# A two-layer encoder trunk on one core: attention issued two sub-steps at a time, with one run of dense products between clusters, and five smaller moves around it

## The chip, the cores and the metric

The kernel runs on one core of a Trainium2 chip. The time is device microseconds (us) of one execution; the median of several executions is what counts. Before the change three timed executions took 2770.01, 2779.59 and 2778.19 us, a median of 2778.19 us.

The engines are TensorE (PE in the profile, its weight loads PEld), VectorE (DVE), ScalarE (ACT), GpSimd (POOL) and the queue of DMA issues (SP).

## The reference, cut to what matters

There are 2048 tokens, 1024 channels, 16 heads of 64. Layer A is a gated pooling mixer, layer B a strictly causal stick-breaking attention; each is followed by an output projection and a gated embedding add.

```python
# layer A
h = rms_norm(x, a_norm);  u, z = split(h @ a_w_in)
x = x + ((group_map(trailing_mean(u) - u) * scale) * silu(z)) @ a_w_out
x = x + (p[0] @ ple_w[0]) * sigmoid(x @ ple_gate_w[0])
# keys and values, once; then layer B
k, v = split(rms_norm(x, kv_norm) @ w_kv);  k = rms_norm_per_head(k)
q, z = split(rms_norm(x, b_norm) @ b_w_in); q = rms_norm_per_head(q)
keep[t, s] = 1 - sigmoid(q_t . k_s / 8)           # s < t
a[t, s]    = sigmoid(q_t . k_s / 8) * prod(keep[t, j] for s < j < t)
o = a @ v
x = x + (o * silu(z)) @ b_w_out
out = x + (p[1] @ ple_w[1]) * sigmoid(x @ ple_gate_w[1])
```

## The kernel before, in words

**Dense products.** Every float32 operand is held as a high and a low part, and each product is three matmuls per 128-row block of the contraction (high by high, high by low, low by high; `product`, line 267, `kvq`, line 632). One product of 128 output rows by 512 tokens is 24 matmuls of 128x512, and it gathers in one of two banks (tile `psd`). Weights come in units of 512 KB (tile `wpair`), nine buffers in a ring. A unit is asked for when the unit nine places ahead of it in `plan` is given back (`give_back`, line 214). On its first use a weight is read raw (`wraw`) and split by ACT (line 176) and DVE (line 177); `keep` stores the split pair in DRAM (`once`), and later uses read the pair. In a chunk, `plan_kvq(s, b)` (line 228) plans half b of the query, key and value weights, eight units of 512 output columns each; the pair is kept if s >= b, so half 0 is raw in chunk 0, and half 1 is raw in chunks 0 and 1.

**Stages.** The tokens go in four chunks of 512. For each chunk the dense stream (`stream`, line 826) runs the mixer, its output projection, the gate, then z of layer B (`gate_z`) and two halves of q, k and v (`kvq`). After the fourth chunk come the output projections and gates of layer B (`post`) for three chunks; that of the last chunk runs alone at the end.

**Attention.** It is laid out in 160 slots (chunk of queries, head, chunk of keys), each of four sub-steps. A sub-step has a front, a turn and a gather. `front` (line 880) makes 128x512 logits with two matmuls (`psl`), ACT takes the sigmoid (line 889), DVE scans the running product along the keys (line 893). `turn` (line 900) transposes one 128-key block of four such tiles into a bank `psa` (two banks), ACT copies the high part `at` (line 908), DVE subtracts the low part (line 910). `gather` (line 912) multiplies both parts by the values (`pso`). The turn of a slot comes `LAG_T` sub-steps behind its front, the gather `LAG_G` behind. The transposes of finished query and key rows (`finish`, line 702, tile `pst`) take the same two `psa` banks.

**What sets the order.** From the first mark on, PE's instructions are held in the order of the program. The loop at line 991 emits, per sub-step, a turn and a front, then half of the step's dense matmuls (`fill`), then a gather and the other half. `rate` (line 965) sets the dense matmuls per sub-step by the chunk of queries: 26.8, 12.9, 7.4 and 5.7. Loads and late steps are hung on a clock that counts dense matmuls (`after`). The other engines' order is set by a scheduler with a timeline of its own. All loads and nearly all stores go through SP's queue, in order.

**Start.** Chunk 0's mixer begins before the sums of squares of x are known: `square_first` (line 413) takes a square on ACT and adds it over channels with four one-column matmuls (`pst<-ones,sq`, eight records in the trace); `norm_first` takes the root and spreads it with four transposes.

## Time and profile before

| | before |
|---|---|
| timed executions, us | 2770.01, 2779.59, 2778.19 |
| the profiled execution's own time, us | 2769.64 |
| its span, first to last instruction, us | 2767.9 |
| mean granted TensorE clock | 0.991 |
| PE busy, us (share) | 2719.8 (98%) |
| DVE, ACT, POOL busy | 65%, 44%, 27% |
| moved by DMA | 684.27 MB, mean 247 GB/s |
| matmul records | 13406 |
| attention, first to last sigmoid, us | 393.1 to 2661.1 |

PE's matmuls overlap, and their ends are modelled; the distance from one start to the next is the price of a matmul, and the duration is not. The granted clock of PE stands in the page as a digit per slice and in the table of windows as a share: 1.00 is full speed, and stretches at half speed pull it down. Busy time of PE at half speed counts as busy.

### The profile page before, as it was taken

The page shows a single profiled execution, that of the slowest core. Times are in us where ns is not written, and L with a number is a line of the kernel's source. Part 1 is how long each engine was busy: PE and PEld are TensorE (multiplying, and loading weights), DVE is VectorE, ACT ScalarE, POOL GpSimd, SP SyncE. Part 2 cuts the span into 40 slices and gives each one's busy share as a digit, 9 for nine tenths or more (in the row PEclk, how much of TensorE's full clock was granted, in tenths as well). Part 3 has the DMA queues.
Part 4 walks back from the last instruction along what each step waited for, and adds up shares of the span by engine and source line. Part 5 has one row for each costly group of instructions (what it writes and reads, how often), then busy time and mean ns, then how long its engine had stood idle before and what let it go on. Part 6 is the DMA issues. An engine that isn't in the chain of part 4 may idle for free.

```text
span 2767.9 us, 37889 instructions
## 1 busy us (share of the span) xinstructions
PE 2719.8 (98%) x13406; PEld 2243.3 (81%) x13406; DVE 1811.1 (65%) x2367; ACT 1229.2 (44%) x2412; POOL 759.0 (27%) x617
## 2 busy tenths in 40 slices
PE   9999989999999999999999999999999999999999
PEld 7878868888877888887778888888888888888887
DVE  5636445644445776655558878776787887887842
ACT  4435543233444334454444445554555444445431
POOL 1345432224432332354223212212211201111101
PEclk8999999999999999999999999999999999999999
DMA  6779888687789878877897676778577765766655
GB/s 223 259 279 346 302 245 279 223 270 246 251 289 321 289 256 272 289 263 249 275 304 235 218 228 208 250 219 265 176 244 239 240 205 184 250 209 211 223 170 184
DMA packets 311306, 684.27 MB, mean 247 GB/s; under 512 B 49222, under 2 KB 81990, under 8 KB 311116
## 3 DMA queue, kind: packets, MB, share of 16 engines
q1 hardware_dynamic: 310540, 681.05, 73.9%
q8 instruction: 106, 1.74, 0.3%
q10 hardware_dynamic: 576, 0.79, 0.1%
q14 instruction: 84, 0.69, 0.1%
HBM read 493.45 MB, written 179.90 MB: 243 GB/s over the span
## 4 chain that ended last, share of the span: by engine, by line
PE 86%; DMA 8%; DVE 2%; ACT 1%; POOL 1%; SPq 1%; issue 1%; ACTq 0%; DVEq 0%; POOLq 0%
PE psd L47 59%; PE psl L47 9%; PE pso L47 9%; PE psa L51 8%; DMA wpair<-once 3%; DMA wraw<-in_w_kv_dram 1%; DMA wraw<-in_b_w_q_dram 1%; PE pst L51 1%; DMA vs<-vr 1%; PE pst L47 1%; DMA kd<-hl 0%; DMA wraw<-in_gate_a_dram 0%; ACT wpair L176 0%; DVE wpair L177 0%; DMA xin<-in_x_dram 0%
## 5 line engine op out<-in xcount | busy, mean ns | idle before, releaser
L893 DVE TENSOR_TENSOR_SCAN pp<-pp,floor 128x512 f32<-128x512 f32 (+3 forms) x640 | 772.9, 1208 | 28.9 <-ACT pp L889 26.9
L910 DVE TENSOR_TENSOR at<-psa,at 128x512 fp32r<-128x512 f32 (+3 forms) x640 | 387.6, 606 | 432.6 <-ACT at L908 429.9
L908 ACT CAST at<-psa 128x512 fp32r<-128x512 f32 (+3 forms) x640 | 333.3, 521 | 726.8 <-PE psa L51 706.1
L47 PE MATMUL psd<-wpair,x 128*128 128x512 f32 x2304 | 615.2, 401 | 25.4 <-DMA wpair<-once 12.8
L47 PE MATMUL psd<-x,wpair 128*128 128x512 f32 x2304 | 606.5, 394 | 1.8 <-ACT x L157 1.6
L47 PEld LDWEIGHTS psd<-wpair,x 128*128 128x128 f32 x2304 | 425.2, 190 | 121.3 <-DMA wpair<-once 20.3
L47 PEld LDWEIGHTS psd<-x,wpair 128*128 128x128 f32 x2304 | 427.1, 188 | 90.0 <-ACT x L157 2.0
L47 PE MATMUL psd<-xp,wpair 128*128 128x512 f32 x1536 | 395.5, 398 | 0.4 <-DVE wpair L177 0.2
L47 PE MATMUL pso<-at,vv 128*128 128x512 f32 (+3 forms) x1280 | 360.9, 363 | 0.0
L889 ACT ACTIVATE pp<-psl 128x512 f32<-128x512 f32 (+3 forms) x640 | 344.6, 538 | 8.7 <-PE psl L47 4.4
L51 PE MATMUL psa<-ident,pp 128*128 128x128 f32 x2176 | 343.7, 273 | 3.0 <-DVE at L910 1.5
L51 PEld LDWEIGHTS psa<-ident,pp 128*128 128x128 f32 x2176 | 275.2, 140 | 84.7 <-DVE pp L893 2.3
L47 PEld LDWEIGHTS psd<-xp,wpair 128*128 128x128 f32 x1536 | 286.9, 191 | 59.6 <-DVE wpair L177 1.2
L47 PE MATMUL psl<-kk,qa 128*128 128x512 f32 (+3 forms) x640 | 283.7, 443 | 0.0
L47 PEld LDWEIGHTS pso<-at,vv 128*128 128x128 f32 x1280 | 240.3, 188 | 53.6
L47 PE MATMUL psl<-kk,qb 128*128 128x512 f32 (+3 forms) x640 | 233.8, 365 | 0.0
L47 PE MATMUL psd<-og,wpair 128*128 128x512 f32 x744 | 208.9, 394 | 0.0
L47 PE MATMUL psd<-mp,wpair 128*128 128x512 f32 x768 | 193.0, 392 | 0.0
L47 PEld LDWEIGHTS psd<-mp,wpair 128*128 128x128 f32 x768 | 142.5, 188 | 29.3
L47 PEld LDWEIGHTS psd<-og,wpair 128*128 128x128 f32 x744 | 137.6, 188 | 28.7
L610 POOL TENSOR_TENSOR xj<-x 128x512 f32<-128x512 f32 x64 | 106.2, 1665 | 149.1 <-DVE sg L621 144.8
L158 POOL TENSOR_TENSOR x<-xr,x 128x512 fp32r<-128x512 f32 x32 | 43.1, 1349 | 329.6 <-ACT x L157 297.1
(118 smaller groups left out, 2655.6 us busy)
## 6 DMA issues: line engine op xcount, KB each, us to landing
wpair<-once SPq DMA_DIRECT2D x468, 512.0 KB
once<-wpair SPq DMA_DIRECT2D x116, 512.0 KB
kk<-kd SPq DMA_DIRECT2D x160, 256.0 KB
vv<-vd SPq DMA_DIRECT2D x160, 256.0 KB
wpair<-wf SPq DMA_DIRECT2D x48, 512.0 KB
once<-kp SPq DMA_DIRECT2D x36, 512.0 KB
qd<-hl SPq DMA_DIRECT2D x64, 256.0 KB
qa<-qd SPq DMA_DIRECT2D x64, 256.0 KB
```

The source lines that it names most:

```text
L47: return held_in_order(nc.tensor.matmul(*a, **k))
L51: return held_in_order(nc.tensor.transpose(*a, **k))
L158: lo.tensor_tensor(out=pr[:, 1], in0=src, in1=f(pr[:, 0]), op=ALU.subtract)
L610: G.tensor_tensor(out=xj, in0=f(x1[o][:, 0]), in1=f(x1[o][:, 1]), op=ALU.add)
L889: A.activation(out=pp[:, r0:], in_=ps[:, :w], func=AF.Sigmoid, scale=-1.0)
L893: V.tensor_tensor_scan(out=pp[:, r0:][:, ::-1], data0=pp[:, r0:][:, ::-1], data1=least, initial=1.0 if st["diag"] else st["carry"][j], op0 ...
L908: A.copy(out=at[:, 0, cs], in_=pt[:, cs])
L910: return lambda: V.tensor_tensor(out=at[:, 1, cs], in0=pt[:, cs], in1=f(at[:, 0, cs]), op=ALU.subtract)
```

## The change

1. The attention loop runs in steps of two sub-steps. Each step emits four gather matmuls, eight transposes, four logit matmuls in one cluster, then DVE's two subtractions and two scans, then one run of `2 * rate` dense matmuls. `LAG_T, LAG_G` are 3 and 4 double steps. The gather of a turned block comes one double step behind its turn; values are loaded two double steps ahead of their first gather. 44 dense matmuls instead of 24 go ahead of the first step.
2. In `kvq`, token blocks 0 and 1 share the second half of block 0's and the first half of block 1's matmuls, as blocks 2 and 3 did before.
3. In chunks 1 and 2, z of layer B goes between the two halves of q, k, v (before: ahead of both; chunk 3 had it between already). There the token norm is then made in `kvq`, and the first two banks are copied out until it is known.
4. The transposes of query and key rows get a time: 28 dense matmuls after the last row, at least 9 apart, and in the attention only inside a dense run, from its 7th matmul to its third last.
5. In the mixer of chunk 0 the squares begin at matmul 15 of the second product instead of 0, five of the eight fall into the third product, and the root and its spreading are apart.
6. The query tile with its halves swapped (`qb`) is made by two ACT copies from `qa`, 14 dense matmuls after its load or at the first front; before, two DMAs read it from DRAM.

The number of PE instructions is the same. ACT has 130 more (128 of them the copies to `qb`), SP 128 fewer.

In the last part of the attention (queries of chunk 3), on PE, one sub-step stood so before (`psa` transposes, `psl` logits, `pso` gathers, `psd` dense):

```order
L51 MATMUL psa<-ident,pp 128x128 x4
L47 MATMUL psl<-kk,qa 128x512
L47 MATMUL psl<-kk,qb 128x512
L47 MATMUL psd<-ple,wpair 128x512 x3
L47 MATMUL pso<-at,vv 128x512 x2
L47 MATMUL psd<-x_22654,wpair 128x512 x3
```

and a double step stands so now:

```order
L47 MATMUL pso<-at,vv 128x512 x4
L51 MATMUL psa<-ident,pp 128x128 x8
L47 MATMUL psl<-kk,qa 128x512
L47 MATMUL psl<-kk,qb 128x512
L47 MATMUL psl<-kk,qa 128x512
L47 MATMUL psl<-kk,qb 128x512
L47 MATMUL psd<-x_22925,wpair 128x512 x3
L47 MATMUL psd<-x_23041,wpair 128x512 x3
L47 MATMUL psd<-x_23140,wpair 128x512 x3
L47 MATMUL psd<-x_23256,wpair 128x512 x2
```

Four short dense runs in two sub-steps have become one of eleven or twelve.

In the mixer of chunk 0, on PE, the first one-column matmuls move back by 15 dense matmuls (`uh` and `ul` belong to the folded weights ahead of it):

```order
 L47 MATMUL psd<-wpair,ul 128x256
 L47 MATMUL psd<-wpair,uh 128x256
-L47 MATMUL psd<-xp,wpair 128x512 x25
+L47 MATMUL psd<-xp,wpair 128x512 x40
 L47 MATMUL pst<-ones,sq 128x1 x4
 L47 MATMUL psd<-xp,wpair 128x512 x3
```

The eight rounds of four such matmuls and three dense ones follow as before.

In the first block of q, k, v of chunk 0, on PE, where x_2151, x_2176, x_2224 and x_2303 are the first four contraction blocks of the activations, token block 1 now begins between the last four contraction blocks of token block 0:

```order
 L47 MATMUL psd<-wpair,x_2224 128x512 x3
 L47 MATMUL psd<-wpair,x_2303 128x512 x3
+L47 MATMUL psd<-wpair,x_2151 128x512 x3
 L47 MATMUL psd<-wpair,x_2349 128x512 x3
+L47 MATMUL psd<-wpair,x_2176 128x512 x3
 L47 MATMUL psd<-wpair,x_2435 128x512 x3
+L47 MATMUL psd<-wpair,x_2224 128x512 x3
 L47 MATMUL psd<-wpair,x_2482 128x512 x3
+L47 MATMUL psd<-wpair,x_2303 128x512 x3
 L47 MATMUL psd<-wpair,x_2570 128x512 x3
-L47 MATMUL psd<-wpair,x_2151 128x512 x3
-L47 MATMUL psd<-wpair,x_2176 128x512 x3
```

Weight units 4 to 7 are first needed at matmuls 15, 21, 27 and 33 of the block; before it was 12, 15, 18 and 21.

```diff
--- before.py
+++ after.py
@@ -27,7 +27,7 @@
 WIN = (2, 4, 8, 16)
 HALO = 16
 UNITS = 9
-LAG_T, LAG_G = 5, 7
+LAG_T, LAG_G = 3, 4
 
 
 def f(ap):
@@ -39,7 +39,7 @@
                  k_norm, b_norm, b_w_q, b_w_z, b_q_norm, b_w_out, ple_a, ple_b, gate_a, gate_b, out):
     nc = tc.nc
     V, A, G = nc.vector, nc.scalar, nc.gpsimd
-    state = {"solo": True, "boot": True, "hold": False, "turn": 0, "lo": 0}
+    state = {"solo": True, "boot": True, "hold": False, "turn": 0, "lo": 0, "since": 0, "until": 0, "next": 0}
 
     class T:
         @staticmethod
@@ -252,11 +252,11 @@
         for b in range(4):
             plan_block("ag", gate_a, b, keep=True)
             plan_block("al", ple_a, b, keep=True, order=PAIRS[:1])
-        if s + 1 == NSUB:
+        if s:
             plan_kvq(s, 0)
         for b in range(4):
             plan_block("zb", b_w_z, b, g_b, True)
-        if s + 1 < NSUB:
+        if not s:
             plan_kvq(s, 0)
         plan_kvq(s, 1)
         if s == 0:
@@ -419,8 +419,11 @@
             T.matmul(chunk[0]["sums"][:, 0, j : j + 1], sq[:, j * P : (j + 1) * P], ones,
                      start=(i + j == 0), stop=(i == KT - 1 and j == 3))
 
+    def root_first():
+        chunk[0]["r1"] = rooted(chunk[0].pop("sums"), "x")
+
     def norm_first():
-        chunk[0]["rb1"] = bcast(rooted(chunk[0].pop("sums"), "x"), "x")
+        chunk[0]["rb1"] = bcast(chunk[0].pop("r1"), "x")
 
     def warm():
         ps = bank("pso", "warm")
@@ -516,13 +519,14 @@
         us = take(4)
         pss = [dense(), dense()]
         yield from product(pss[0], us, ck["x"], 0, 0)
-        hooks = {3 * i: [lambda i=i: square_first(i)] for i in range(KT)}
+        hooks = {15 + 3 * i: [lambda i=i: square_first(i)] for i in range(3)}
         yield from hooked(product(pss[1], us, ck["x"], P, 1), hooks)
-        while later:
-            later.pop(0)()
         us = take(4)
         zs = []
-        hooks = {8: [norm_first], 9: [lambda: zs.extend(silu(ps, ck["rb1"]) for ps in pss)]}
+        hooks = {3 * i: [lambda i=i: square_first(3 + i)] for i in range(5)}
+        hooks[12] += [root_first] + later
+        later.clear()
+        hooks |= {21: [norm_first], 22: [lambda: zs.extend(silu(ps, ck["rb1"]) for ps in pss)]}
         for k in range(2):
             ps = dense()
             yield from hooked(product(ps, us, ck["x"], k * P, k), {} if k else hooks)
@@ -625,14 +629,16 @@
 
     lag = []
 
-    STEPS = [(j, kt) for j in range(2) for kt in range(KT)]
-    STEPS += [(2, 0), (2, 1), (2, 2), (2, 3), (3, 0), (2, 4), (3, 1), (2, 5), (3, 2), (2, 6), (3, 3), (2, 7)]
-    STEPS += [(3, kt) for kt in range(4, KT)]
+    STEPS = []
+    for j in (0, 2):
+        STEPS += [(j, kt) for kt in range(4)]
+        STEPS += [(j + i, kt + 4 * (1 - i)) for kt in range(4) for i in (1, 0)]
+        STEPS += [(j + 1, kt) for kt in range(4, KT)]
 
     def kvq(s, kind, b):
         ck = chunk[s]
         us = take(KT)
-        banks = {}
+        banks, early = {}, []
         for j, kt in STEPS:
             tk = slice(j * P, (j + 1) * P)
             if kt == 0:
@@ -644,14 +650,27 @@
                 if j == 3 and wh:
                     give_back()
                 yield
-            if lag and (j, kt) in ((1, 2), (1, 6), (2, 2), (3, 1)):
-                lag.pop(0)()
+            calm = state["solo"] or 7 <= state["since"] <= state["until"] - 3
+            if lag and calm and time["now"] >= max(state["next"], lag[0][0]):
+                lag.pop(0)[1]()
+                state["next"] = time["now"] + 9
             if kt < KT - 1:
                 continue
+            done = [(j, banks.pop(j))]
             if "r2" not in ck:
+                qs = row("qs")
+                A.copy(out=qs, in_=done[0][1])
+                early.append((j, qs))
+                if j == 0:
+                    continue
                 ck["r2"] = token_norm(ck["acc2"], "y")
-            rj = ck["r2"][:, j : j + 1]
-            (valued if kind == "v" else keyed)(s, kind, b, j, banks.pop(j), rj)
+                done = early
+            if kind == "v" and j == 3:
+                while lag:
+                    lag.pop(0)[1]()
+            for i, ps in done:
+                rj = ck["r2"][:, i : i + 1]
+                (valued if kind == "v" else keyed)(s, kind, b, i, ps, rj)
 
     def valued(s, kind, b, j, ps, rj):
         vr = row("vr")
@@ -716,7 +735,7 @@
                       in_=f(hl)[e * HD : (e + 1) * HD])
 
         for m in range(4):
-            lag.append(lambda m=m: finish(m))
+            lag.append((time["now"] + 28, lambda m=m: finish(m)))
 
     def every(gen, n, side):
         i = 0
@@ -786,13 +805,13 @@
         ple = load_ple(0, s)
         yield from gate_steps(x1, ple, put_x2(s))
         ck["side"] = prep(s + 1) if s + 1 < NSUB else iter(())
-        if s + 1 < NSUB:
+        if not s:
             yield from every(gate_z(s), 48, ck["side"])
         for kind in "qkv":
             yield from every(kvq(s, kind, 0), 48, ck["side"])
         after(60, lambda: marks.add((s, 0)))
-        if s + 1 == NSUB:
-            yield from gate_z(s)
+        if s:
+            yield from every(gate_z(s), 48, ck["side"])
 
     def second_part(s):
         ck = chunk[s]
@@ -854,9 +873,15 @@
     def load_q(c, h):
         qa, qb = qryt("qa"), qryt("qb")
         nc.sync.dma_start(out=f(qa), in_=qd[c][h].rearrange("l d n -> (l d) n"))
-        for l in range(2):
-            nc.sync.dma_start(out=f(qb)[(1 - l) * HD : (2 - l) * HD], in_=qd[c][h][l])
-        return qa, qb
+        left = [0, 1]
+
+        def swap():
+            while left:
+                l = left.pop()
+                A.copy(out=qb[(1 - l) * HD : (2 - l) * HD], in_=qa[l * HD : (l + 1) * HD])
+
+        after(14, swap)
+        return qa, qb, swap
 
     def load_k(kc, h):
         kk = keyt("kk")
@@ -882,7 +907,8 @@
         r0 = W5 - w
         ps = bank("psl", "psl")
         qs = slice(j * P, (j + 1) * P)
-        (qa, qb), kk = st["q"], st["k"]
+        (qa, qb, swap), kk = st["q"], st["k"]
+        swap()
         T.matmul(ps[:, :w], qa[:, qs], kk[:, :w], start=True, stop=False)
         T.matmul(ps[:, :w], qb[:, qs], kk[:, :w], start=False, stop=True)
         pp = ppt("pp")
@@ -971,8 +997,7 @@
     until((0, 0))
     state["solo"], state["hold"] = False, True
     begin(0)
-    begin_v(0)
-    for _ in range(24):
+    for _ in range(44):
         next(run)
     owed = 0.0
     count = 0
@@ -980,39 +1005,38 @@
     def fill(share):
         nonlocal owed, count
         owed += share
+        state["since"], state["until"] = 0, int(owed)
         while owed >= 1.0:
+            state["since"] += 1
             next(run, None)
             owed -= 1.0
             count += 1
             if count % 54 == 0 and kept and (1, 1) in marks:
                 keep(*kept.pop(0))
 
-    scan = None
-    for n in range(4 * len(slots) + LAG_G):
-        i, j = divmod(n, 4)
-        x_ = rate(i)
-        i2, j2 = divmod(n - LAG_T, 4)
-        low = turn(active[i2], j2) if 0 <= i2 < len(slots) else None
-        due, scan = scan, None
+    for n in range(2 * len(slots) + LAG_G + 1):
+        i, j = divmod(n, 2)
+        i2, j2 = divmod(n - LAG_T, 2)
+        i3, j3 = divmod(n - LAG_G, 2)
+        both = lambda h: (2 * h, 2 * h + 1)
+        if 0 <= i3 < len(slots):
+            for kt in both(j3):
+                gather(active[i3], kt)
+            if j3:
+                active.pop(i3)
+        lows = [turn(active[i2], kt) for kt in both(j2)] if 0 <= i2 < len(slots) else []
+        scans = []
         if i < len(slots):
             if j == 0 and i + 1 < len(slots):
                 begin(i + 1)
             elif j == 0:
                 load_heads(NSUB - 1, 6)
-            if j == 3 and i + 1 < len(slots):
-                begin_v(i + 1)
-            scan = front(active[i], j)
-        if due:
-            due()
-        if low:
-            low()
-        fill(x_ / 2)
-        i3, j3 = divmod(n - LAG_G, 4)
-        if 0 <= i3 < len(slots):
-            gather(active[i3], j3)
-            if j3 == 3:
-                active.pop(i3)
-        fill(x_ / 2)
+            scans = [front(active[i], jj) for jj in both(j)]
+        if j2 == 1 and -1 <= i2 < len(slots) - 1:
+            begin_v(i2 + 1)
+        for do in lows + scans:
+            do()
+        fill(2 * rate(i))
     for _ in run:
         pass
     pass_time(100)
```

## The prediction

> **What bounds the kernel now.** I read the page's busy rows and its chain of waits first, then PE's waits, then windows over the stretches in which PE is not full.

> ```profile
> span 2767.9 us, 37889 instructions
> PE 2719.8 (98%) x13406; PEld 2243.3 (81%) x13406; DVE 1811.1 (65%) x2367; ACT 1229.2 (44%) x2412; POOL 759.0 (27%) x617
> PE 86%; DMA 8%; DVE 2%; ACT 1%; POOL 1%; SPq 1%; issue 1%; ACTq 0%; DVEq 0%; POOLq 0%
> PE psd L47 <- DMA wpair<-once: 12.8, 13, 2.1
> PE psd L47 <- ACT wpair L176: 11.4, 6, 3.3
> PE pst L51 <- DVE hl L158: 2.7, 1, 2.7
> PE pst L51 <- DVE qs L696: 1.9, 2, 1.6
> PE pst L51 <- ACT ss L364: 1.6, 1, 1.6
> ```

> PE sets the end: the chain runs through it for 86%. The change takes no matmul away, so a gain can only come from idle time of PE, from time at half clock, and from the distance between matmuls. The windows (length, then busy us and count per engine, granted clock, DMA share, GB/s) tell how much of the first two there is and where:

> ```profile
> 24.00:48.00 24.00, 24.00 (x91) 21.25 (x91) 6.12 (x12) 9.02 (x19) 1.24 (x2) 0.54 0.71 257
> 190.00:202.00 12.00, 8.97 (x30) 5.91 (x29) 3.85 (x5) 4.55 (x8) 5.46 (x5) 0.86 0.93 320
> 360.00:405.00 45.00, 37.11 (x154) 27.95 (x154) 21.03 (x31) 20.92 (x36) 16.39 (x16) 0.96 0.82 239
> 740.00:775.00 35.00, 31.24 (x150) 24.50 (x149) 16.74 (x25) 13.21 (x24) 11.56 (x11) 1.00 0.78 263
> 800.00:875.00 75.00, 66.93 (x303) 53.01 (x302) 40.85 (x61) 36.77 (x68) 22.12 (x20) 0.93 0.95 318
> 1250.00:1335.00 85.00, 76.86 (x374) 62.30 (x373) 41.38 (x57) 36.60 (x73) 25.58 (x21) 0.96 0.79 265
> 1355.00:1405.00 50.00, 46.13 (x222) 36.41 (x221) 27.40 (x38) 22.27 (x43) 14.38 (x14) 0.97 0.78 273
> 2100.00:2640.00 540.00, 540.00 (x2796) 447.69 (x2796) 436.73 (x521) 262.83 (x521) 73.81 (x48) 1.00 0.65 217
> ```

> In each row I take length less PE's busy time as idle, and length times (1 - clock) as lost to the clock. The five windows from 360 to 1405 are the q, k, v blocks of chunks 0, 1 and 2. They lose 7.9 + 1.8, 3.8 + 0, 8.1 + 5.3, 8.1 + 3.4 and 3.9 + 1.5 us, 43.8 together. The start loses 11.0 to the clock. The last row, the queries of chunk 3, has no idle PE at all, while DVE is 81% busy. There the change can only shorten the distance between matmuls, or lose.

> **The change part by part.** First the squares at the start.

> ```profile
> 23.29 1.05 PE L47 MATMUL pst<-ones,sq 128*128 128x1 f32 x8 [2.64 <-ACT sq L417]
> 24.20 0.95 PE L47 MATMUL psd<-xp,wpair 128*128 128x512 f32 x3
> 24.99 0.95 PE L47 MATMUL pst<-ones,sq 128*128 128x1 f32 x8
> 25.81 1.63 PE L47 MATMUL psd<-xp,wpair 128*128 128x512 f32 x3
> 28.80 1.63 PE L47 MATMUL psd<-xp,wpair 128*128 128x512 f32 x3
> 27.05 0.91 ACT L176 ACTIVATE wpair<-wraw,g_a 128x256 fp32r<-128x256 f32 x2 [0.18 <-PE psd L47]
> 2681.45 81.64 PE psd L47 x360
> ```

> PE waits 2.64 us for the first square, and right after that the clock is at half: a round of three dense and eight one-column matmuls takes 1.61 us (24.20 to 25.81), then 2.99 (25.81 to 28.80). Fifteen dense matmuls now stand ahead, at 81.64 / 360 = 0.227 us each (the last row, of the chain in order of time) 3.4 us. ACT gets two weight splits ahead of its first square, 0.91 us by the ACT row. So the wait goes. Whether the clock then stays up is open. The rounds at full clock hold 3 x 0.227 = 0.68 us of dense matmul in 1.61, 42%, and rounds at half clock did not bring it back: that came only behind the last of them. The bounds are 2.6 us (the rounds pull the clock down themselves) and 2.6 + 11.0 = 13.6. I take 8, between the two. [...]

> Next the weights in q, k, v. PE's waits there are for weights in DMA or in ACT's split behind DMA (the last row is the list of waits from 1250 to 1335).

> ```profile
> 806.05 3.65 PE L47 MATMUL psd<-wpair,x 128*128 128x512 f32 x9 [3.32 <-ACT wpair L176]
> 834.60 1.58 PE L47 MATMUL psd<-wpair,x 128*128 128x512 f32 x3 [1.67 <-ACT wpair L176]
> 838.55 3.26 PE L47 MATMUL psd<-wpair,x 128*128 128x512 f32 x7 [2.37 <-ACT wpair L176]
> 769.26 0.97 PE L47 MATMUL psd<-wpair,x 128*128 128x512 f32 x3 [0.97 <-DMA wpair<-once]
> 771.20 0.97 PE L47 MATMUL psd<-wpair,x 128*128 128x512 f32 x3 [0.97 <-DMA wpair<-once]
> PE psd L47 <- DMA wpair<-once: 5.3, 4, 2.1
> ```

> Half 1 of chunk 1 is raw, so the wait ahead of 806.05 is at its entry, from v of half 0 to q of half 1. With z between them, its units come one by one behind z's. That boundary goes in chunks 1 and 2: 3.3 us, 1.4 behind it at half clock (nine matmuls in 3.65 us, of 2.2 at full), and 1.6 in chunk 2 (an estimate: some third of that window's 5.3 us), 6.3. What takes its place, gate to q and v to z, has the less crowded of the two blocks on one side; I price it at nothing. The other boundaries stay, but units 4 to 7 are needed 3, 6, 9 and 12 matmuls later. At 26.8 dense matmuls and 1.4 us of attention a sub-step one dense matmul costs about 0.28 us, at 12.9 about 0.33, so the last unit gets 3.4 to 4 us more. The waits at 769 and 771 are one unit (three matmuls) apart, a shortage that builds up over the units, which this covers; those at 834 and 838 are at the first units of a block, which gain nothing. DMA is 78 to 95% busy in these windows, which speaks against full relief. Of 43.8, 6.2 are the transposes' (below) and 6.3 the boundary. Of the 31.3 left the bounds are none and all; I take half, 15.7, since both kinds of wait are there. Together 22.

> The transposes of finished heads wait 2.7 + 1.9 + 1.6 = 6.2 us, for a bank or a row. They now come 28 dense matmuls (6.4 us) after the row, not beside a cluster, and 9 apart. Bounds 0 and 6.2; I take 6.

> Then the runs of dense matmuls. These are two sub-steps' worth of the last part before:

> ```profile
> 2401.13 0.60 PE L51 MATMUL psa<-ident,pp 128*128 128x128 f32 x4
> 2401.48 0.48 PE L47 MATMUL psl<-kk,qa 128*128 128x512 f32 x1
> 2402.72 0.62 PE L47 MATMUL pso<-at,vv 128*128 128x512 f32 x2
> 2403.87 0.60 PE L51 MATMUL psa<-ident,pp 128*128 128x128 f32 x4
> 2401.76 0.59 ACT L908 CAST at<-psa 128x512 fp32r<-128x512 f32 x1 [1.67 <-PE psa L51]
> L893 DVE TENSOR_TENSOR_SCAN pp<-pp,floor 128x512 f32<-128x512 f32 x448 | 621.6, 1387 | 28.4 <-ACT pp L889 26.6
> L910 DVE TENSOR_TENSOR at<-psa,at 128x512 fp32r<-128x512 f32 x448 | 307.4, 686 | 322.9 <-ACT at L908 321.5
> L925 ACT COPY os<-pso 64x512 f32<-64x512 f32 x64 | 37.2, 582 | 42.2 <-PE pso L47 41.5
> ```

> A sub-step takes 2.74 us (2401.13 to 2403.87). It holds ten matmuls of 512 columns, 2.27 us at 0.227, and four transposes: they and the first logits matmul run from 2401.13 until 2401.80 or so, 0.67, so 0.44 without that matmul. That makes 2.71, and 0.03 to 0.04 us a sub-step lie in the changes of kind, some 20 us over 640 sub-steps. About half of the changes go. Bounds 0 and 14; I take 8. So the clustering alone is a small thing.

> What it may cost is distance. A low part `at` was needed two and a half sub-steps behind its transposes (LAG 5 to 7 and half a step), 6.8 us; now it is one double step, 5.4. DVE must do two subtractions (2 x 0.69) and two scans (2 x 1.39) in that, 4.15 us, and its share of dense evictions, which bring the 437 of 540 us. From the first `psa` bank (0.2 us behind the fourth transpose), an ACT copy of 0.59 and a subtraction of 0.69, twice, the second low part stands about 2.8 us behind the first transpose. The gather that needs it comes about 5 us behind, so some 2 us of cover are left where there were nearly five. DVE's evictions of 0.7 to 1.6 us fit in that once, not twice. Bounds 0 and 0.35 us on each of 224 double steps (128 of the last part, 96 of the one before), 78; I take 6, since only two evictions in one step use up the cover.

> The values are loaded two double steps ahead of use, four sub-steps; the keys had the same four sub-steps before, and no wait of `psl` for `kk` stands in PE's list. I price that, 20 more dense matmuls ahead of the first step and the longer drain at nothing: the same PE work in another place. The 128 copies to `qb`, by the nearest row (L925, 64x512, 0.582 us) 74 us of ACT, lie beside PE, ACT being 49% busy in the last part; they take 16.8 MB of 684 off DMA. If `qa` is late, everything behind the copy on ACT waits, sigmoids and `at` first: at 1 us for each of 64 heads 64 us less the slack, so at most some 50.

> The sum: -8 -22 -6 -8 +6 = -38 us, on the profiled execution's own 2769.6 (its span is 2767.9, so 1.7 lie around it) 2731.6. The median of the runs stands 8.6 above that execution, so I forecast 2740.

> **The rivals.**
> - All of the shortage goes and the clock stays up: -13.6 - 37.6 - 6.2 - 14 = -71, 2707. For it: each wait in the list is short, 3.3 us at most, against 3.4 to 4 us of relief. Against it: first units get none, and DMA is 95% busy from 800 to 875.
> - Bandwidth, not timing, sets the waits: then the 15.7 are not there, the start gives 2.6, and the transposes and the runs 3 each. -2.6 - 6.3 - 3 - 3 + 6 = -9, 2769. For it stand the DMA shares; against it 263 to 273 GB/s in three of the windows where 318 is to be had.
> - DVE takes over as the bound in the last two parts: the low part misses its gather by 0.35 us in each of 224 double steps, +78 against -44, 2812. It decides from 0.2 us a step (44 / 224) on. For it: DVE at 81%, and four operations of 4.15 us in 5.4. Against it: the four and the mean eviction stay below the step.
> - The cluster does nothing by itself and the copy to `qb` blocks ACT on a late `qa`: +50 - 38, 2790. Against it: 14 dense matmuls, 3.2 us and at most times a cluster, lie ahead of it, and only chunk 0's heads are so close.

> **How the numbers follow.** Forecast 0.5; all goes 0.15; bandwidth 0.18; DVE 0.11; `qa` 0.06. The forecast's own range, by its bounds without the far ends, is 2718 to 2765. The whole range leaves out part of the best case and most of DVE's: 2704 to 2788. A measurement of this kernel can tell about 0.5%, 13.9 us, from no change: faster is below 2764, slower above 2792. Forecast and best case are nearly all faster, 0.62 of 0.65; of bandwidth a third, 0.06. Slower is DVE's 0.09 and 0.03 of `qa`; the rest is the same.

> **What would show it.** Right: PE's list without waits on L158 and L696 for `pst`; no L176 wait at the entry of half 1 in chunk 1; the waits on `wpair<-once` about halved; a granted clock of 1.0 in part of 24 to 48 us; one sub-step of the last part at 2.72 or less. Wrong: `pso` waiting for `at` L910 (now another line) in more than a few double steps, `psl` waiting for `qb`, idle PE between 1500 and 2640, or the same waits on weights at the same boundaries.

## The result

The changed kernel takes 2748.78 us, median of four runs (2741.94 to 2751.33), against 2776.39 for the kernel before on the same chips (the three executions given above and one of 2774.58). The ratio is 0.990, with a 95% interval of 0.9873 to 0.9926: 27.6 us faster, where 38 were forecast. The profiled execution is the fastest of the four, 2741.94 us.

The first lines are the page's span, busy row and chain shares, then PE's waits, then windows of the changed kernel: six that the prediction quoted of the kernel before, and the last two parts of the attention. They stand at the same times as before; the changed kernel is 14 us ahead from the start on, and more later, so they hold nearly the same work, not quite.

```profile
span 2740.2 us, 38112 instructions
PE 2691.3 (98%) x13406; PEld 2248.5 (82%) x13406; DVE 1789.6 (65%) x2367; ACT 1274.3 (47%) x2542; POOL 743.2 (27%) x617
PE 84%; DMA 6%; DVE 3%; ACT 2%; POOL 2%; issue 1%; SPq 1%; ACTq 0%; DVEq 0%; POOLq 0%
PE pso L47 <- DVE at L936: 5.4, 7, 2.1
PE psd L47 <- ACT qs L708: 5.1, 3, 3.1
PE pst L51 <- DVE qs L715: 3.8, 3, 2.3
PE pst L51 <- DVE at L936: 3.2, 5, 1.1
PE psa L51 <- DVE hl L158: 3.0, 3, 1.8
...
PE psa L51 <- DVE hl L731: 2.6, 3, 1.2
PE psl L47 <- ACT qs L708: 2.3, 1, 2.3
...
PE psd L47 <- DMA wpair<-once: 0.6, 2, 0.3
24.00:48.00 24.00, 24.00 (x154) 21.59 (x154) 11.03 (x20) 12.74 (x25) 5.18 (x7) 1.00 0.76 299
360.00:405.00 45.00, 39.56 (x172) 31.65 (x171) 24.56 (x37) 22.59 (x38) 14.96 (x13) 0.92 0.80 231
740.00:775.00 35.00, 35.00 (x176) 29.76 (x175) 16.58 (x23) 14.62 (x29) 14.02 (x11) 1.00 1.01 349
800.00:875.00 75.00, 70.21 (x343) 57.96 (x342) 44.72 (x64) 40.46 (x76) 17.71 (x16) 0.98 0.89 308
1250.00:1335.00 85.00, 85.00 (x432) 71.97 (x431) 44.84 (x63) 39.69 (x82) 29.52 (x24) 1.00 0.85 309
1355.00:1405.00 50.00, 50.00 (x257) 42.14 (x256) 29.20 (x40) 24.51 (x50) 14.23 (x12) 1.00 0.96 326
1500.00:2640.00 1140.00, 1129.93 (x5866) 950.03 (x5865) 872.84 (x1071) 565.12 (x1153) 191.74 (x145) 1.00 0.65 213
```

The chain still runs through PE. Three things are to be seen. The waits for weights are all but gone: 12.8 us on `wpair<-once` are 0.6 now, and the 11.4 on L176 have no row left. In their place stand many waits for what ACT and DVE make, at most 5.4 us in sum each. And the start runs at full clock, 1.00 from 24 to 48 us where it was 0.54.

The span splits into three parts by two numbers of each profile: idle PE (span less PE's busy time), clock loss (span times one less the mean granted clock), and the rest, which is PE busy at full clock. Before: 2767.9 = 48.1 idle + 24.9 clock (0.991) + 2694.9 rest. After: 2740.2 = 48.9 idle + 11.0 clock (0.996) + 2680.3 rest. So the clock gave 13.9 us, the distance between matmuls about 14.6, and **idle PE nothing at all**: 24 us of waits on weights went and as many came elsewhere. The clock is printed to three places, so each clock part is good to 1.4 us, and busy time rests on modelled ends of matmuls; the same split over all kernels below shows what can be trusted.

Where the new waits stand shows by stages. In the queries of chunk 0 idle PE fell only from 16.9 to 13.9 us, by these rows of before and after; in those of chunk 1 it fell from 12.3 to 6.4, and in those of chunks 2 and 3 it rose from 2.8 to 8.2 and from 0.2 to 6.4.

```profile
384.20:869.40 485.20, 468.27 (x2216) 383.81 (x2214) 248.93 (x351) 190.71 (x373) 159.19 (x142) 0.99 0.80 263
375.00:854.60 479.60, 465.74 (x2225) 387.62 (x2224) 246.33 (x349) 206.15 (x403) 162.87 (x142) 0.99 0.78 263
```

### The profile page after: what moved, and what is told of

Read it like the earlier page. It is cut to its first block, busy times and chain, and to the rows that moved or that the text cites. A ratio compares the mean times of both kernels' runs of the same rounds, so it can differ in the third digit from the quotient of the medians.

```text
span 2740.2 us, 38112 instructions
## 1 busy us (share of the span) xinstructions
PE 2691.3 (98%) x13406; PEld 2248.5 (82%) x13406; DVE 1789.6 (65%) x2367; ACT 1274.3 (47%) x2542; POOL 743.2 (27%) x617
## 4 chain that ended last, share of the span: by engine, by line
PE 84%; DMA 6%; DVE 3%; ACT 2%; POOL 2%; issue 1%; SPq 1%; ACTq 0%; DVEq 0%; POOLq 0%
PE psd L47 58%; PE pso L47 9%; PE psl L47 9%; PE psa L51 8%; DMA qa<-qd 1%; DMA xin<-in_x_dram 1%; PE pst L51 1%; DMA wraw<-in_w_kv_dram 1%; DMA vs<-vr 1%; DVE pp L919 1%; POOL rq L150 1%; DVE at L936 1%; DMA wpair<-once 0%; PE pst L47 0%; SPq L66 0%
## 5 line engine op out<-in xcount | busy, mean ns | idle before, releaser
L919 DVE TENSOR_TENSOR_SCAN pp<-pp,floor 128x512 f32<-128x512 f32 (+3 forms) x640 | 736.2, 1184 | 8.2 <-ACT pp L915 6.6
L47 PE MATMUL psd<-wpair,x 128*128 128x512 f32 x2304 | 565.5, 396 | 6.0 <-ACT qs L708 5.1
L936 DVE TENSOR_TENSOR at<-psa,at 128x512 fp32r<-128x512 f32 (+3 forms) x640 | 361.3, 604 | 313.3 <-ACT at L934 311.3
L47 PE MATMUL psd<-x,wpair 128*128 128x512 f32 x2304 | 553.9, 391 | 6.1 <-ACT sg L621 2.3
L47 PEld LDWEIGHTS psd<-x,wpair 128*128 128x128 f32 x2304 | 431.7, 188 | 99.3 <-DVE sg L624 3.1
L47 PEld LDWEIGHTS psd<-wpair,x 128*128 128x128 f32 x2304 | 428.8, 190 | 97.7 <-ACT qs L708 7.5
L934 ACT CAST at<-psa 128x512 fp32r<-128x512 f32 (+3 forms) x640 | 303.4, 524 | 405.1 <-PE psa L51 403.0
L47 PE MATMUL psd<-xp,wpair 128*128 128x512 f32 x1536 | 361.6, 391 | 0.4 <-DVE wpair L177 0.2
L47 PEld LDWEIGHTS psd<-xp,wpair 128*128 128x128 f32 x1536 | 286.1, 188 | 61.3 <-DVE wpair L177 1.4
L47 PE MATMUL pso<-at,vv 128*128 128x512 f32 (+3 forms) x1280 | 315.1, 365 | 7.6 <-DVE at L936 5.4
L915 ACT ACTIVATE pp<-psl 128x512 f32<-128x512 f32 (+3 forms) x640 | 315.8, 548 | 2.8 <-PE psl L47 2.3
L51 PE MATMUL psa<-ident,pp 128*128 128x128 f32 x2176 | 292.3, 273 | 5.6 <-DVE hl L158 3.0
L47 PEld LDWEIGHTS pso<-at,vv 128*128 128x128 f32 x1280 | 231.3, 188 | 61.4 <-DVE at L936 10.5
L51 PEld LDWEIGHTS psa<-ident,pp 128*128 128x128 f32 x2176 | 252.5, 141 | 35.2 <-DVE hl L158 3.8
L47 PE MATMUL psl<-kk,qa 128*128 128x512 f32 (+3 forms) x640 | 257.5, 407 | 2.3 <-ACT qs L708 2.3
L47 PE MATMUL psl<-kk,qb 128*128 128x512 f32 (+3 forms) x640 | 233.2, 364 | 0.0
L47 PE MATMUL psd<-og,wpair 128*128 128x512 f32 x744 | 182.2, 391 | 2.0 <-DVE os L952 1.4
L47 PE MATMUL psd<-mp,wpair 128*128 128x512 f32 x768 | 179.3, 390 | 0.0
L47 PEld LDWEIGHTS psd<-mp,wpair 128*128 128x128 f32 x768 | 143.8, 188 | 30.1
L47 PEld LDWEIGHTS psd<-og,wpair 128*128 128x128 f32 x744 | 138.8, 188 | 32.8 <-DVE os L952 1.8
L960 POOL TENSOR_TENSOR os<-os,zt 128x512 f32<-128x512 f32 x32 | 49.7, 1553 | 345.2 <-ACT os L959 325.0
```

The costliest lines, as they stand in the source:

```text
L47: return held_in_order(nc.tensor.matmul(*a, **k))
L51: return held_in_order(nc.tensor.transpose(*a, **k))
L915: A.activation(out=pp[:, r0:], in_=ps[:, :w], func=AF.Sigmoid, scale=-1.0)
L919: V.tensor_tensor_scan(out=pp[:, r0:][:, ::-1], data0=pp[:, r0:][:, ::-1], data1=least, initial=1.0 if st["diag"] else st["carry"][j], op0 ...
L934: A.copy(out=at[:, 0, cs], in_=pt[:, cs])
L936: return lambda: V.tensor_tensor(out=at[:, 1, cs], in0=pt[:, cs], in1=f(at[:, 0, cs]), op=ALU.subtract)
```

## The experiments

Most are the change with one part undone or one number altered; three combine such edits, and qb_busy adds work to u_qb. Times are medians and ratios those to the kernel before on the same chip. The last three columns are the split above for the profiled execution of each.

| kernel | us | ratio, 95% | idle | clock loss | rest |
|---|---|---|---|---|---|
| the change | 2748.78 | 0.990, 0.9873 to 0.9926 | 48.9 | 11.0 | 2680.3 |
| u_squares | 2759.54 | 0.9959, 0.9945 to 0.9973 | 52.4 | 24.8 | 2679.4 |
| thin2 | 2756.69 | 0.9942, 0.9929 to 0.9954 | 53.6 | 22.0 | 2679.3 |
| u_pair | 2760.13 | 0.995, 0.9938 to 0.9963 | 57.1 | 16.6 | 2685.3 |
| u_z | 2748.65 | 0.9919, 0.9906 to 0.9931 | 52.3 | 16.5 | 2678.1 |
| u_lag | 2759.92 | 0.9956, 0.9942 to 0.997 | 62.9 | 22.1 | 2679.5 |
| u_double | 2744.76 | 0.9909, 0.9896 to 0.9923 | 36.6 | 24.8 | 2690.3 |
| single_thick | 2742.04 | 0.9884, 0.9868 to 0.9901 | 36.9 | 8.2 | 2695.3 |
| single_qb_thick | 2738.21 | 0.9876, 0.9861 to 0.9891 | 33.4 | 5.5 | 2692.2 |
| u_qb | 2735.72 | 0.9874, 0.986 to 0.9887 | 48.1 | 13.7 | 2678.5 |
| qb_late | 2746.89 | 0.9909, 0.9895 to 0.9923 | 53.9 | 11.0 | 2680.6 |
| qb_thick | 2735.12 | 0.9861, 0.9847 to 0.9874 | 45.0 | 5.5 | 2679.6 |
| qb_busy | 2771.76 | 0.9995, 0.9986 to 1.0003 | 62.1 | 27.7 | 2678.7 |

One execution of each was profiled, and not always a typical one: that of the change is the shortest of its executions, those of u_lag, u_double and u_qb are the longest of theirs. The clock loss of u_lag and u_double above all is that of one execution; in their others the granted clock was 0.995 to 0.997.

**The start: u_squares and thin2.** u_squares puts the squares back where they were:

```diff
-        hooks = {15 + 3 * i: [lambda i=i: square_first(i)] for i in range(3)}
+        hooks = {3 * i: [lambda i=i: square_first(i)] for i in range(KT)}
...
-        hooks = {3 * i: [lambda i=i: square_first(3 + i)] for i in range(5)}
-        hooks[12] += [root_first] + later
...
```

> The change without its part 5: the squares start at matmul 0 of the second product again, root and spreading together. Theory 1 (the start gains by the wait and by the clock that then stays up): the start loses 13 to 14 us again, the granted clock falls to half between about 24 and 48 us, all later stages stay; ratio to before 0.994 to 0.996. Theory 2 (the clock has another cause): only the wait of 2.6 us returns, ratio 0.990 to 0.992.

thin2 keeps them late, but leaves two dense matmuls between the square rounds instead of three:

```diff
-        hooks = {15 + 3 * i: [lambda i=i: square_first(i)] for i in range(3)}
+        hooks = {15 + 2 * i: [lambda i=i: square_first(i)] for i in range(5)}
...
-        hooks = {3 * i: [lambda i=i: square_first(3 + i)] for i in range(5)}
-        hooks[12] += [root_first] + later
+        hooks = {1 + 2 * i: [lambda i=i: square_first(5 + i)] for i in range(3)}
+        hooks[12] = [root_first] + later
```

> The change with two dense matmuls instead of three between the squares' one-column matmuls; the first square stands behind the same 40 dense matmuls, so PE does not wait for it. [...] Theory 2 (only a wait of PE brings the clock down): the clock stays up, ratio 0.990.

Both lose what the start had won: the ratios go up by 0.0059 and 0.0042, 16 and 12 us. In u_squares the wait of 2.6 us for the first square is back. In thin2 no wait of PE stands in the 6 us ahead of the rounds or in them, and the clock falls all the same: 0.64 from 24 to 48 us, where the change has 1.00. These are rows of PE's timeline, of the change, of thin2, of one execution of u_double and of qb_thick (four dense a round):

```profile
24.94 0.95 PE L47 MATMUL psd<-xp,wpair 128*128 128x512 f32 x3
26.54 0.96 PE L47 MATMUL psd<-xp,wpair 128*128 128x512 f32 x3
```

```profile
24.60 0.71 PE L47 MATMUL psd<-xp,wpair 128*128 128x512 f32 x2
25.95 0.71 PE L47 MATMUL psd<-xp,wpair 128*128 128x512 f32 x2
27.48 1.20 PE L47 MATMUL psd<-xp,wpair 128*128 128x512 f32 x2
30.04 1.20 PE L47 MATMUL psd<-xp,wpair 128*128 128x512 f32 x2
```

```profile
24.10 1.05 PE L47 MATMUL pst<-ones,sq 128*128 128x1 f32 x8 [0.40 <-ACT sq L417]
25.01 0.94 PE L47 MATMUL psd<-xp,wpair 128*128 128x512 f32 x3
26.71 1.63 PE L47 MATMUL psd<-xp,wpair 128*128 128x512 f32 x3
29.69 1.63 PE L47 MATMUL psd<-xp,wpair 128*128 128x512 f32 x3
```

```profile
24.74 1.16 PE L47 MATMUL psd<-xp,wpair 128*128 128x512 f32 x4
26.54 1.16 PE L47 MATMUL psd<-xp,wpair 128*128 128x512 f32 x4
```

At 0.227 us a dense matmul, its share of a round is 0.43 in the change (0.68 of 1.60), 0.34 in thin2 (0.45 of 1.35), 0.50 in qb_thick (0.91 of 1.80). After two rounds at 0.34, of 1.35 and 1.53 us, the clock is halved: the third takes 2.56. So the rounds at 0.34 pulled the clock down by themselves, and with them the longer lead alone was not enough. At 0.43 the profiles divide by the wait ahead of the rounds. In the six with three dense matmuls a round and no wait between 20 and 50 us (the change, u_qb, u_z, u_pair, qb_late, u_lag) the clock holds, 1.00 from 24 to 48 us; in those with a wait it falls, after 2.6 us in u_squares and in the kernel before (0.51 and 0.54), and after 0.40 us in u_double (0.55), where the rounds then take 2.98. That execution of u_double took 2753.97 us against 2742.92 to 2747.72 for the other four, which show a clock of 0.995 or 0.996 where it shows 0.991. No run varies the wait by itself, so that the 0.40 us brought the clock down is likely, not shown. Where an edge lies is not measured either: without a wait, 0.34 fell and 0.43 held.

**The weights: u_pair and u_z.** u_pair gives `kvq` its old order of token blocks; u_z puts z of layer B back ahead of both halves:

```diff
-    STEPS = []
-    for j in (0, 2):
-        STEPS += [(j, kt) for kt in range(4)]
...
+    STEPS = [(j, kt) for j in range(2) for kt in range(KT)]
+    STEPS += [(2, 0), (2, 1), (2, 2), (2, 3), (3, 0), (2, 4), (3, 1), (2, 5), (3, 2), (2, 6), (3, 3), (2, 7)]
...
```

> The change without its part 2: token blocks 0 and 1 one after the other again. Theory 1 (pairing covers the late units): waits on weights of 8 us or more return in the q, k, v blocks of chunks 0 to 2; ratio 0.993 to 0.995. Theory 2 (z between the halves and the longer runs cover them): less than 3 us; ratio 0.990.

```diff
-        if s:
+        if s + 1 == NSUB:
             plan_kvq(s, 0)
...
```

> The change without its part 3: z ahead of both halves in chunks 1 and 2 again. Theory 1: the boundary between the halves returns with 4 to 8 us of waits on weights in the attention of chunks 0 and 1; ratio 0.992 to 0.993. Theory 2 (pairing alone covers it): less than 2 us; ratio 0.990.

Without the pairing the wait is back, in nineteen short pieces, and idle and clock loss grow by 8 and 6 us (the first row is from u_pair's list of PE's waits). Its price is 0.005 of the ratio, 14 us. Without z between the halves 3.9 us of it return in four pieces (the second row, of u_z's list), and the ratio is higher by 0.0019, 5 us, which lies within the intervals: z's share stays unresolved. The long dense runs are not what took the waits away: u_double, with the short runs of before, has 1.4 us of waits on `wpair<-once` and 0.5 on L176.

```profile
PE psd L47 <- DMA wpair<-once: 10.1, 19, 1.6
```

```profile
PE psd L47 <- DMA wpair<-once: 3.9, 4, 2.4
```

**The double step: u_double, u_lag, single_thick.** u_double undoes it and its rule of distances together:

```diff
-LAG_T, LAG_G = 3, 4
+LAG_T, LAG_G = 5, 7
...
-            calm = state["solo"] or 7 <= state["since"] <= state["until"] - 3
-            if lag and calm and time["now"] >= max(state["next"], lag[0][0]):
+            if lag and (j, kt) in ((1, 2), (1, 6), (2, 2), (3, 1)):
...
-    for n in range(2 * len(slots) + LAG_G + 1):
+    for n in range(4 * len(slots) + LAG_G):
...
```

> The change without its parts 1 and 4: single sub-steps as before, heads' transposes at their old places; squares, pairing, z and the copied qb stay. Theory 1 (pairing and z took the waits on weights away): PE's waits on weights stay below 5 us in all, the waits of pso for at go, the runs' 8 us are lost; ratio 0.988 to 0.992, about as the change. Theory 2 (the long dense runs took the waits on weights away): 15 us or more of waits on wpair return; ratio 0.995 or more.

u_lag keeps the double step and undoes the rule alone, the second pair of lines above.

> The change without its part 4: the pieces put off by the token mixer's end are taken at the four old places of a value or key unit (after the third and seventh k-tile of two token blocks' products and so on) and are not flushed at the end of a value unit; everything else as in the change. Theory 1 (the rule of calm distances is worth nothing measurable): ratio 0.989 to 0.991, within 3 us of the change. Rival (the rule earns its place, since pieces at fixed places fall beside the copies of half-heads): ratio 0.993 or more, with waits of PE for L158 and L731 above 8 us in sum (5.6 in the change). Second rival (the rule itself makes the waits for the low parts at L936, 8.6 us in the change, by bunching VectorE's pieces): those fall below 4 us and the ratio is 0.987 or less.

single_thick is u_double with four dense matmuls a round, so that the clock of the start is out of the comparison:

```diff
-        hooks = {15 + 3 * i: [lambda i=i: square_first(i)] for i in range(3)}
+        hooks = {15 + 4 * i: [lambda i=i: square_first(i)] for i in range(3)}
...
```

> The change without the double step and its rule of distances (parts 1 and 4), with four dense products per round of squares and with the query copies kept: of the change remain the paired token blocks, the z between the halves, the later squares and the copies. Theory 1 (the copies cost about 7 us with any step, the double step nothing): ratio 0.989 to 0.991, beside 0.9876 for the same kernel with the second query tile by transfer. Rival (the copies cost only with double steps, where two heads' worth of work shares a stretch of ScalarE): ratio 0.986 to 0.988. Second rival (the single step is worse once the clock of the start is left out): 0.992 or more.

The double step is worth nothing that can be measured: 0.9909 and 0.9884 without it, 0.990 with it, and with `qb` by DMA (below) 0.9876 without and 0.9861 with it; the intervals overlap. The table says why. With single steps the rest is 2690 to 2695 us, with double steps 2678 to 2681 in every kernel but u_pair: about 12 us less between matmuls, and u_lag (2679.5) shows that the step brings this and not the rule of distances. But idle PE is 33 to 37 with single steps and 45 or more with double ones: the 12 us come back as waits. Here are the busy rows of single_thick and of the change's counterpart in the last comparison, qb_thick:

```profile
span 2740.4 us, 37867 instructions
PE 2703.5 (99%) x13406; PEld 2232.5 (81%) x13406; DVE 1813.8 (66%) x2367; ACT 1306.9 (48%) x2542; POOL 755.6 (28%) x617
```

```profile
span 2730.1 us, 38131 instructions
PE 2685.1 (98%) x13406; PEld 2244.2 (82%) x13406; DVE 1789.7 (66%) x2367; ACT 1198.0 (44%) x2414; POOL 744.4 (27%) x617
```

u_lag was a miss of my theory: I expected nothing, and it costs 0.0056, 16 us by the ratios and 11 by the medians, with an interval clear of the change's. So the rule of calm distances is what keeps the double step from costing more than it saves. Its profiled execution has 14 us more idle PE than the change's. The rival named waits of `psa` for split parts, above 8 us; they are 7.9 where the change has 5.6. What grows most in the list are the waits of the transposes for their rows, 8.4 us (the first line) where the change has 3.8. The other lines, of ACT and then of PE, show one place of its timeline:

```profile
PE pst L51 <- DVE qs L710: 8.4, 5, 3.5
2084.84 1.24 ACT L876 CAST qb<-qa 64x512 fp32r<-64x512 f32 x2 [5.25 <-DMA qa<-qd]
2086.11 1.07 ACT L929 CAST at<-psa 128x512 fp32r<-128x512 f32 x2
2080.36 1.03 PE L51 MATMUL psa<-ident,pp 128*128 128x128 f32 x8
2086.75 0.50 PE L47 MATMUL pso<-at,vv 128*128 128x512 f32 x1 [2.38 <-ACT at L929]
2088.73 1.91 PE L51 MATMUL psa<-ident,pp 128*128 128x128 f32 x8
```

The two query copies stand at ACT's head for 5.25 us until `qa` has landed. Behind them wait the high parts `at`, whose `psa` banks PE had filled by 2081.4, and so the gather waits 2.38 us. Right behind it the eight transposes take 1.91 us instead of 1.03, 0.54 of the speed. This place is not the rule's: the change has one like it, quoted below, with a wait of 1.98 us, and there the clock is 1.00 from 2060 to 2068 us and the transposes behind the wait take 1.03. These 0.88 us add to what the wait costs, but what makes up u_lag's whole loss is not shown.

**The query copies: u_qb, qb_late, qb_busy, and two kernels in combination.** u_qb loads `qb` by DMA again, as before:

```diff
-        left = [0, 1]
-        def swap():
...
-        after(14, swap)
-        return qa, qb, swap
+        for l in range(2):
+            nc.sync.dma_start(out=f(qb)[(1 - l) * HD : (2 - l) * HD], in_=qd[c][h][l])
+        return qa, qb, lambda: None
```

> The change without its part 6: qb is read by two DMAs again. Theory 1 (ACT stands behind the copies, which wait for qa): ACT's 108 us of waiting for qa go, PE's waits for ACT (sg L621, qs L708, at L934; 12 us with the change) fall below 4, waits on weights grow by 3 at most; ratio 0.986 to 0.989. Theory 2 (the DMAs saved are worth more): waits on weights grow by 8 us or more; ratio 0.991 or more.

It is faster than the change, 0.9874 against 0.990, about 7 us, though the intervals overlap. The sign that I had named came only in part: PE's waits for ACT (sg L621, qs L708, at) are 9.3 us instead of 12.2, not below 4, and its waits on weights grow by 2.9. The change's own rows say what may cost this: a group row, its row among ACT's waits, and one place in the last part.

```profile
L881 ACT CAST qb<-qa 64x512 fp32r<-64x512 f32 x128 | 79.1, 618 | 109.3 <-DMA qa<-qd 108.1
ACT qb L881 <- DMA qa<-qd: 108.1, 53, 4.8
2061.68 1.24 ACT L881 CAST qb<-qa 64x512 fp32r<-64x512 f32 x2 [4.82 <-DMA qa<-qd]
2062.95 1.07 ACT L934 CAST at<-psa 128x512 fp32r<-128x512 f32 x2
2063.58 0.50 PE L47 MATMUL pso<-at,vv 128*128 128x512 f32 x1 [1.98 <-ACT at L934]
```

ACT stands 108.1 us behind `qa`, at 53 places. At one of them, the one quoted, PE waits for the `at` behind the copy, its only wait on that line in the whole list; that DVE and PE are held up later at others is possible, and not shown. There `at` starts at 2062.95, as the copies end (2061.68 and 1.24). Two runs were to part the standing from the copies' own 79 us, and neither could. qb_late moved the copies from 14 steps behind the load to 40:

```diff
-        after(14, swap)
+        after(40, swap)
```

> The change with one number altered: the two copies that make a head's second query tile are queued on ScalarE 40 steps after the load of its first tile instead of 14, so that the tile should have landed by then; as many copies as in the change. Theory 1 (ScalarE loses by standing behind the transfer: 108.1 us of its idle time in the change's profile is L881 waiting for the first query tile): that wait falls below 20 us, and the time goes most of the way to that of the kernel whose second tile comes by transfer: ratio to the kernel before 0.987 to 0.989. Rival (the copies' own 128 x 618 ns on ScalarE cost the time, wherever they stand): the wait falls, but the ratio stays at 0.990 or above. Second rival: the copies now come too late and the first product of a head waits for them: PE waits for L881 in sum above 5 us and the ratio is 0.991 or more.

The wait did not fall, it is 113.7 us, and the time is the change's. What is written late is not run late: the copies still start 2.5 to 8.3 us behind the issue of their load, as in the change (2.5 to 7.7). The scheduler sets the order on ACT by a timeline of its own, and here it did not follow the program. As a second measurement of nearly the same kernel this run is of use: its interval, 0.9895 to 0.9923, lies clear of u_qb's, 0.986 to 0.9887. qb_busy adds to u_qb three copies a head that wait for nothing:

```diff
+    dump = cp.tile([P, 320], mybir.dt.bfloat16, name="dump")
...
+                A.copy(out=dump[(1 - l) * HD : (2 - l) * HD], in_=floor[l * HD : (l + 1) * HD, 0:320])
...
```

> The kernel with the second query tile by transfer, and in addition three copies of 64x320 numbers on ScalarE for every head, from a constant tile into one that nobody reads, queued where the change queues its two copies: about as much copying (192 copies against 128 of 64x512), but no transfer to wait for. Theory 1 (the price of the change's copies is that ScalarE stands behind the transfer of the first query tile, 108.1 us of idle time): the spare copies cost next to nothing and the ratio to the kernel before is 0.986 to 0.989, as with the transfers alone (0.9874). Rival (the copies' own 79 us on ScalarE delay what comes behind them): the ratio is 0.990 or above, as with the change.

It took 2771.76 us, ratio 0.9995 (0.9986 to 1.0003). This is the rival's number, but not for its reason: the window rows of the spare copies show 164 of the 192 ahead of 140 us and none behind 400.

```profile
0.00:140.00 140.00, 75.14 (x164) 0.88 0.55 196
...
400.00:2769.00 2369.00, 0.00 (x0) 1.00 0.73 245
```

Work that waits for nothing was drawn into the start, and there PE waited for ACT: 5.6 us for the folded weights (`uh`), 4.1 for a square, 3.1 for weight splits. By the first matmul of layer A's output projection (`psd<-mp`), at 162.1 us against 126.9 in u_qb's profile, 35 us are lost, and some 7 of them come back later. So it stays open whether the copies cost by standing or by working. With single steps no price of the copies can be measured: single_thick, which has them, is at 0.9884, between what its theory and its rival gave, and 2 us above single_qb_thick (0.9876), the same kernel without them; the intervals overlap.

The combinations were run for the sum of these readings:

> The change with qb by DMA (part 6 undone) and four dense matmuls between the squares. Theory: the clock never falls in the squares (0.91 of 1.81 us is 0.50), in no execution, and ACT does not stand behind qa; ratio 0.985 to 0.988, and the spread of the runs gets smaller. Rival: three dense matmuls were enough, ratio as without the copies, 0.987, with the same spread.

> Single sub-steps and the heads' transposes at their old places (parts 1 and 4 undone), qb by DMA, four dense matmuls between the squares; only pairing, z and the later squares are left of the change. Theory 1 (the double step is worth nothing on balance: its 8 us go into waits for low parts): ratio 0.985 to 0.988, within 4 us of the double step with the same start and qb. Theory 2 (it is worth its runs): 0.990 or more.

qb_thick, the change with `qb` by DMA and four dense matmuls a round, is the fastest kernel of the study, 2735.12 us and 0.9861, though not clear of u_qb. single_qb_thick, with nothing left of the change but the pairing, z and the later squares, reaches 0.9876: no worse than the whole change. Four dense matmuls add nothing that can be told over three where three hold (u_qb 0.9874); single_thick, u_double with four, shows a clock of 1.00 from 24 to 48 us where u_double shows 0.55, but whether four are a margin behind a wait is not shown.

## Why the prediction was right, and where it was not

The forecast, 2740, lies 9 us under the median and in the right direction for mostly right reasons; the terms were less right than their sum. By the runs, roughly, the start gave 14 us, the weights 19 (u_pair 14, u_z 5 and unresolved), the longer runs 12; the double step's waits took 12 and the copies 7. That is 26 in sum, near the 27.6 measured. The forecast had too little for the start and the runs, and too little for the new waits and the copies. That these errors offset each other is luck.

- **Start, forecast 8 between bounds of 2.6 and 13.6.** It is the upper bound: 13.8 us by the first matmul of layer A's output projection (141.0 us before, 127.2 after), 16 by u_squares. Mis-sized: I let the thin rounds pull the clock down half of the time, and rounds of three dense matmuls hold it in all six profiles in which no wait stands ahead of them. That rounds can pull it down by themselves was right at 0.34 (thin2). The lower bound, the wait alone, is refuted: the part gave 13.8.
- **Weights, forecast 22.** Waits of 24.2 us became 0.6. The window rows agree: 740 to 775, 1250 to 1335 and 1355 to 1405 have no idle PE and a clock of 1.00, where they lost 15.8 idle and 4.9 to the clock. The step that failed is "half of the rest" at the other boundaries, the first units of a block being out of reach: nearly all waits on weights went. But the time did not all come back. The row of 360 to 405 still loses 5.4 us idle and 3.6 to the clock, 9.0 where it lost 9.7, and that of 800 to 875 loses 4.8 and 1.5, to waits for rows of queries and keys (qs L715 3.4, qs L708 1.4). Undoing parts 2 and 3 costs 14 and 5 us, 19 in sum, near the 22. And the bandwidth rival is refuted in its own place: DMA moved 349 and 326 GB/s in two of these windows, where it had moved 263 and 273. The pairing did most of it (u_pair).
- **Transposes, forecast 6.** Nothing. Waits of `pst` for `qs` are 3.8 us where 1.9 stood; those of `psa` for the split parts of finished heads (L158, L731), 5.6 us, were 0.2. The `pst` waits for L158 fell from 2.7 to 1.1, no more. A list without them was named as a sign beforehand, and it failed. Yet the rule has a worth that I did not see: it is what makes the double step bearable (u_lag).
- **Runs of dense matmuls, forecast 8 of at most 14.** About 12 to 14.6 by the rest column. The mechanism was right and the size taken low: by the prediction's own rows some 20 us lie in the changes of kind, and about half of that is 10, where it takes 8. The sign named for it, a sub-step of 2.72 us or less in the last part, came but is small, as the starts of three clusters of the change show:

```profile
2397.02 1.10 PE L47 MATMUL pso<-at,vv 128*128 128x512 f32 x4
2402.25 1.10 PE L47 MATMUL pso<-at,vv 128*128 128x512 f32 x4
2407.39 0.98 PE L47 MATMUL pso<-at,vv 128*128 128x512 f32 x4
```

  These double steps of 5.23 and 5.14 us have eleven dense matmuls each; with twelve, as in the sub-steps quoted of before, they would be 5.37 to 5.46, some 2.7 a sub-step against 2.74.
- **New waits, forecast 6 of at most 78.** This is the term that was wrong most. Single and double steps differ by 12 us of idle PE, on top of the waits of finished rows and copies; in all about 24 us of new waits filled the place of the old. Low parts `at` make 8.6 of them (L936, 12 waits), far from a wait in each of 224 steps, so DVE is not the bound: the rival at 2812 fell. But idle PE between 1500 and 2640, which I named as a sign against me, is 10.1 us where it was 1.6 (1140 less 1138.39 before). In the same window u_qb has 6.5, qb_thick 5.9 and single_qb_thick 2.3, so the copies and the double step seem to have a part in it, some 4 us each. The row of before:

```profile
1500.00:2640.00 1140.00, 1138.39 (x5881) 943.18 (x5880) 900.53 (x1085) 560.92 (x1111) 217.04 (x155) 1.00 0.68 222
```

- **Priced at nothing.** For the copies to `qb` this failed. Their 74 us of ACT were right (79.1), and `qa` late as well, but "at most 50 us" did not come in: about 7. The cover of 14 dense matmuls did not hold: ACT stood for `qa` at 53 places. Of the values' earlier load and the longer drain no run says anything by itself.

One wait is older than it looks. "ACT qs L708", 7.4 us with PE as its victim, is ACT evicting a block of keys or queries late; at 377 to 382 us it is late because the splits of raw weights ahead of it stand for their DMA; that is 5.4 of the 7.4 us (rows of ACT, then PE):

```profile
379.02 0.72 ACT L176 ACTIVATE wpair<-wraw,gains 128x512 fp32r<-128x512 f32 x1 [1.51 <-DMA wraw<-in_w_kv_dram]
381.39 0.67 ACT L708 ACTIVATE qs<-psd,r 128x512 f32<-128x512 f32 x1
382.11 6.57 PE L47 MATMUL psd<-wpair,x 128*128 128x512 f32 x18 [3.13 <-ACT qs L708]
```

So some of the shortage of weights is still there, under another name.

## What to carry to other kernels

Split the span into idle, clock loss and the rest before and after, not the wait list alone: a change can save in one and pay in another, as the double step does here, 12 us each way, and only the sum is on the clock. A DMA share of 0.78 did not make the shortage a bandwidth limit here: spreading the same weights over more time took these waits away, with more bytes moved per us (349 and 326 GB/s where it had been 263 and 273). The copies on ACT that stood for a transfer held up what was queued behind them, as the rows of `qb` and `at` show (4.82 us on ACT, and behind them 1.98 on PE); with double steps, letting the DMA write both tiles was 7 us faster here. And undo the parts of a change one by one: three small moves of this one, without the step that it is named after, came out no worse than the whole.

## What the runs showed of the hardware

```profile
24.00:48.00 24.00, 23.90 (x93) 21.36 (x94) 5.47 (x12) 8.51 (x19) 1.24 (x2) 0.55 0.68 264
```

```profile
1049.03 0.62 ACT L157 CAST x<-xr 128x512 fp32r<-128x512 f32 x1
```
